# Seeding a PSUM bank with the first product, and a new order of the seven products, in a two-layer hybrid decoder

## The chip, the cores and the metric

One Trainium2 chip, all 8 cores. Each core runs the same program on one prompt sequence of 2048 tokens and 16 sample tokens (2064 columns); the cores share nothing but the memory. The metric is the device time of the slowest core in microseconds (us). Most executions agree within 0.3%. In some, one pair of cores or a whole die runs at a lower granted TensorE clock and the time is longer by some per cent or more; those runs are called slow and are not compared with anything here. A milder form, a pair of cores or a die at a clock of 0.97 to 0.98, still counts as fast in the ratios; it is named where it occurs, and there single stages are read from the undisturbed cores.

## The reference

Two layers of: half a SwiGLU feed-forward, a token mixer, half a second SwiGLU feed-forward. Only the feed-forwards are touched.

```python
D_MODEL, SEQ, BATCH, DEPTH, D_FF = 1024, 2048, 8, 2, 2816

def swiglu(x, w_gate, w_up, w_down):
    return (jax.nn.silu(x @ w_gate) * (x @ w_up)) @ w_down

def hybrid_layer(x, ...):
    h = x + 0.5 * swiglu(rms_norm(x, ffn1_norm), ffn1_w_gate, ffn1_w_up, ffn1_w_down)
    ...                                  # mixer: chunk MLP and short convolution, gated, h = h + m @ w_out
    h = h + 0.5 * swiglu(rms_norm(h, ffn2_norm), ffn2_w_gate, ffn2_w_up, ffn2_w_down)
    return h, new_buf, v
```

## The kernel before

The engines' names below: PE multiplies matrices, DVE and POOL work on vectors, ACT evaluates functions and copies. The token columns on a core make three pairs of blocks (344 + 344 columns). The 2816 hidden rows make 22 row blocks, in groups of 6, 8 and 8 ("groups 0, 1, 2").

**Gate and up.** For one row block and one pair of token blocks (a "unit"), gate and up for both token blocks form a 2 x 2 product of blocks. It is done as Strassen and Winograd do it, with seven products in place of eight. A product is four matmuls of 344 columns. Three PSUM banks y, z and w collect sums of products. A unit is spread over 17 slots; a new one begins every 7 slots, so at any time two to three are in flight and every slot has one product:

```python
t = 7 * u
put(t, begin)
put(t, lambda: (prod(1, "y", True), snap(ta, taR)))                     # ACT copies y to ta
put(t + 1, lambda: (prod(2, "z", True), add(ta, taR, "z"), free("z")))  # DVE: ta += z
put(t + 3, lambda: prod(7, "w", True))
put(t + 4, lambda: (prod(6, "y", False), snap(tb, tbR)))                # ACT copies y to tb
put(t + 9, lambda: (prod(5, "y", False), snap(tc, tcR)))                # ACT copies y to tc
put(t + 10, lambda: (add(tc, tcR, "w"), silu(ta, taR)))                 # DVE: tc += w; ACT: silu
put(t + 12, lambda: (prod(3, "y", False), out1(), free("y")))           # DVE: act = y * ta
put(t + 13, lambda: (prod(4, "w", False), end(), add(tb, tbR, "w"), free("w")))
put(t + 15, lambda: silu(tb, tbR))
put(t + 16, out2)                                                       # DVE: act = tc * tb
```

`end()` lets POOL make the weight differences (tiles T) of a later row block. Products 3, 5 and 6 use token differences (tiles S), products 4 to 6 weight differences (T). Product 7 uses one difference of each kind too, made in place: tokens in `nh` by DVE, weights in `ring` by POOL. In the rows of the profile, `pb` is a PSUM bank, `ring` the weights as loaded, `nh` the normed tokens and `D` the weight differences of the down-projection. `out2` has both inputs in SBUF; the other DVE operations of a unit have one in PSUM.

**Down.** The down-projections of groups 0 (three row pairs) and 1 (four row pairs) are also done with seven products, in three "thirds" (pairs of token blocks) of 14 steps (7 products, 2 halves of the output). DVE adds finished pairs of PSUM banks to h; four of the adds (three in the first third) go through an ACT copy and POOL instead. DVE also makes differences of activations (t3, t2 and two more) in every third. The down-projection of group 2 is plain.

```python
class Down:
    ORDER = ((1, "y", 0, 0), (2, "z", 0, 0), (7, "w", 4, 1), (6, "y", 4, 0), (4, "w", 4, 0), (5, "y", 4, 1), (3, "y", 0, 1))
    OTHER = ((2, 0), (7, 1), (4, 0), (3, 0))          # added by way of ACT and POOL
    ...
    def step(self, p, i, bank, blk, tok, dq, part=None):
        ...                                           # matmuls into the pair of banks
        add_half(tw[2], sz, hc, [tw[0][1], tw[1][1]] + hR, hR)   # DVE: h += half the pair
```

**Background work.** Norm work (squares on ACT, sums, normed tiles nh and token differences on DVE) is queued and let through at a fixed rate while the first units of a feed-forward run:

```python
if t % 7 in ((0, 3) if early and t < 84 else (2, 5)):
    bg.run(1)
```

Three stages, called "starts" here, have this load: group 0 of the second feed-forward of layer 0, of the first of layer 1, and of the second of layer 1 (start 1, 2, 3; at about 930, 1370 and 2270 us).

## Time and profile before

| | before |
|---|---|
| time, three runs beforehand | 2726.13 us (2725.81 to 2726.48) |
| PE busy | 97% of the span |
| DVE, ACT, POOL busy | 74%, 41%, 41% |
| PE time lost above the pace of its matmuls, in what the change touches | 69 us of 2722 |

A matmul of 344 columns starts 146 ns after the one before it when nothing holds PE up. So "stall" here always means: the distance between two starts in the trace, less that pace. From the same starts comes a ledger of stages, used throughout: a stage begins with its first matmul and ends where the next begins; the number is the median over the eight cores of one profiled execution. It is worked out from the trace, and is not a view of it. The ledger before, us:

```
beginning                                     116.2
start 1 / start 2 / start 3          78.4 / 81.5 / 78.8
gate/up of the other eight groups             806.3   ("regular")
very first down stage                          44.7
first thirds of the three later three-pair down stages   50.2
later thirds of the same                       85.8
four-pair down stages                         210.3
plain down, mixer, end                       1168.7
```

The rows of the profile that carry the reading are in the prediction below.

### The profile page before, as it was taken

To read this page: it belongs to the slowest core of one execution; us is meant where nothing else is said; L and a number is where in the kernel's file an instruction comes from. 1 tells how busy PE (TensorE), PEld (TensorE's weight loads), DVE (VectorE), ACT (ScalarE), POOL (GpSimd) and SP (SyncE) were. 2 spreads that over 40 slices of the span, in tenths; PEclk is the share of its full clock that TensorE was granted. 3 is DMA by queue.
4 is the path that set the end of the run, shared out by engine and by line. 5 is a ranking of instruction groups with operands and counts; after the bars stand their busy time and mean duration, and the time that the engine had idled before them with its cause. 6 is when DMAs were issued, how large, how long until landed. Compare 5 with 4: busy or idle time off the path is not lost.

```text
span 2722.9 us, 42526 instructions; the slowest of 8 cores (2718.5 to 2723.2 us)
## 1 busy us (share of the span) xinstructions
PE 2645.4 (97%) x16464; PEld 1592.5 (58%) x16464; DVE 2014.5 (74%) x3337; ACT 1113.3 (41%) x2188; POOL 1116.7 (41%) x1165
## 2 busy tenths in 40 slices
PE   8999999999999999999999999999999999999997
PEld 4466665566555565666555666646665555566664
DVE  5776667877787887676888676598768879866656
ACT  4244353523442443525353534453225224343356
POOL 1466536111221537563547646331112115575623
PEclk8999999999999999999999999999999999999999
DMA  7332323444364322222023313314444442232313
GB/s 173 47 47 34 49 36 65 70 71 70 57 101 75 60 41 45 40 47 43 13 32 47 62 25 60 69 32 78 71 70 76 82 74 37 47 55 32 55 32 125
DMA packets 87977, 159.66 MB, mean 59 GB/s; under 512 B 9376, under 2 KB 18464, under 8 KB 87488
## 3 DMA queue, kind: packets, MB, share of 16 engines
q0 software_dynamic: 74880, 136.35, 32.3%
q1 hardware_dynamic: 12464, 19.94, 2.3%
q8 instruction: 130, 2.13, 0.3%
q14 instruction: 71, 0.58, 0.1%
q10 hardware_dynamic: 432, 0.66, 0.1%
HBM read 284.49 MB, written 8.86 MB: 108 GB/s over the span
## 4 chain that ended last, share of the span: by engine, by line
PE 82%; DVE 13%; ACT 2%; issue 2%; POOL 1%; DMA 0%; SPq 0%; ACTq 0%; DVEq 0%; POOLq 0%
PE pb L288 45%; PE pb L284 37%; DVE h L266 3%; DVE nh L266 3%; DVE act L258 2%; DVE y L258 1%; ACT sq L246 1%; DVE acc L258 1%; DVE S L258 0%; DVE sq L258 0%; DMA h<-xT 0%; DVE tb L258 0%; DVE tc L258 0%; POOL sq L258 0%; DVE vb L258 0%
## 5 line engine op out<-in xcount | busy, mean ns | idle before, releaser
L272 POOL DMA_DIRECT2D ring<-wpk x456 | 247.5, 549 | 989.6 <-PE pb L284 529.6
L284 PE MATMUL pb<-nh,ring 128*128 128x384 f16 (+2 forms) x3360 | 607.8, 340 | 2.8 <-DVE nh L266 2.7
L288 PE MATMUL pb<-nh,ring 128*128 128x344 f16 x2952 | 510.4, 310 | 5.6 <-DVE nh L258 3.8
L284 PEld LDWEIGHTS pb<-nh,ring 128*128 128x128 f16 x3360 | 326.2, 98 | 258.1 <-issue 7.5
L266 DVE SCALAR_TENSOR_TENSOR h<-pb,h 128x688 f32<-128x688 f32 (+4 forms) x368 | 332.0, 911 | 136.4 <-PE pb L284 68.3
L288 PEld LDWEIGHTS pb<-nh,ring 128*128 128x128 f16 x2952 | 288.5, 98 | 150.1 <-DVE nh L258 4.8
L288 PE MATMUL pb<-S,T 128*128 128x344 f16 x1968 | 368.2, 310 | 3.8 <-POOL T L258 2.4
L288 PEld LDWEIGHTS pb<-S,T 128*128 128x128 f16 x1968 | 191.8, 98 | 100.8 <-POOL T L258 3.8
L246 ACT ACTIVATE ta<-pb 128x344 f32<-128x344 f32 x246 | 112.4, 457 | 321.2 <-PE pb L288 301.9
L258 DVE TENSOR_TENSOR ta<-pb,ta 128x344 f32<-128x344 f32 x246 | 126.8, 516 | 144.0 <-PE pb L288 142.1
L284 PE MATMUL pb<-act,ring 128*128 128x384 f16 (+3 forms) x1280 | 224.4, 336 | 3.0 <-DVE h L266 2.7
L288 PE MATMUL pb<-act,ring 128*128 128x344 f16 x1344 | 211.5, 310 | 12.2 <-DVE h L266 12.2
L258 DVE TENSOR_TENSOR act<-pb,ta 128x344 f16<-128x344 f32 x246 | 126.8, 515 | 127.0 <-PE pb L288 120.9
L258 POOL TENSOR_TENSOR T<-ring,T 128x512 f16<-128x512 f16 x164 | 212.7, 1297 | 12.9
L246 ACT ACTIVATE sq<-h 128x768 f32<-128x768 f32 (+3 forms) x140 | 121.7, 876 | 213.7 <-DVE h L266 193.8
L288 PE MATMUL pb<-nh,T 128*128 128x344 f16 x984 | 184.4, 310 | 11.5 <-DVE tc L258 7.1
L258 POOL TENSOR_TENSOR h<-h,cp 128x688 f32<-128x688 f32 x88 | 146.5, 1667 | 111.1 <-ACT cp L246 110.9
L266 DVE SCALAR_TENSOR_TENSOR nh<-h,cv,acc 128x384 f16<-128x384 f32 (+2 forms) x240 | 185.8, 816 | 7.1 <-ACT acc L246 3.6
L258 DVE TENSOR_TENSOR act<-tc,tb 128x344 f16<-128x344 f32 x246 | 181.0, 736 | 6.7 <-ACT tb L246 6.7
L288 PE MATMUL pb<-S,ring 128*128 128x344 f16 x984 | 184.4, 310 | 1.2 <-ACT tc L246 0.9
L284 PEld LDWEIGHTS pb<-act,ring 128*128 128x128 f16 x1280 | 123.5, 99 | 104.3 <-issue 9.6
L246 ACT ACTIVATE cp<-pb 128x688 f32<-128x688 f32 x88 | 65.4, 743 | 281.4 <-PE pb L288 281.4
(127 smaller groups left out, 3884.7 us busy)
## 6 DMA issues: line engine op xcount, KB each, us to landing
ring<-wpk POOLq DMA_DIRECT2D x456, 256.0 KB, 5.3
ext<-wpk POOLq DMA_DIRECT2D x64, 256.0 KB, 5.7
yT<-y SPq DMA_DIRECT2D x6, 768.0 KB, 3.6
h<-xT SPq DMA_DIRECT2D x4, 768.0 KB, 7.8
h<-xT SPq DMA_DIRECT2D x2, 1024.0 KB, 8.5
yT<-y SPq DMA_DIRECT2D x2, 1024.0 KB, 3.9
h<-xT SPq DMA_DIRECT2D x2, 800.0 KB, 8.1
h<-xT SPq DMA_DIRECT2D x4, 384.0 KB, 8.9
```

The lines of the kernel that those rows point to most:

```text
L246: return lambda e: e.activation(out=out, in_=in_, func=func, scale=scale)
L258: return lambda e: e.tensor_tensor(out=out, in0=in0, in1=in1, op=op)
L266: return lambda e: e.scalar_tensor_tensor(out=out, in0=in0, scalar=scalar, in1=in1, op0=op0, op1=op1)
L272: return lambda e: e.dma_start(out=out, in_=in_)
L284: return lambda e: e.matmul(out, lhsT=lhsT, rhs=rhs, start=start, stop=stop)
L288: return lambda e: e.matmul(out, lhsT=lhsT, rhs=rhs, start=start, stop=stop, skip_group_check=True)
```

## The change

Intent: take DVE work off. Product 1 is copied by ACT into bank z, before product 2 accumulates on it there, so the sum of products 1 and 2 arises in PSUM and DVE's add is gone. For this product 2 comes two slots later and product 7 takes its place. The third temporary tc is filled the other way round: bank w is copied soon after product 7, and y is added to it after product 5; product 4 comes before product 3. The down-projection gets the same seed and one read of h less. The silu now reads bank z early. Background work runs three times in seven slots, instead of twice, at the start of the first feed-forwards.

```diff
-                    put(t, lambda: (prod(1, "y", True), snap(ta, taR)))
-                    put(t + 1, lambda: (prod(2, "z", True), add(ta, taR, "z"), free("z")))
-                    put(t + 3, lambda: prod(7, "w", True))
-                    put(t + 4, lambda: (prod(6, "y", False), snap(tb, tbR)))
-                    put(t + 9, lambda: (prod(5, "y", False), snap(tc, tcR)))
-                    put(t + 10, lambda: (add(tc, tcR, "w"), silu(ta, taR)))
-                    put(t + 12, lambda: (prod(3, "y", False), out1(), free("y")))
-                    put(t + 13, lambda: (prod(4, "w", False), end(), add(tb, tbR, "w"), free("w")))
-                    put(t + 15, lambda: silu(tb, tbR))
+                    put(t, lambda: (prod(1, "y", True), seed()))
+                    put(t + 1, lambda: (prod(7, "w", True), snap(tc, tcR, "w")))
+                    put(t + 3, lambda: prod(2, "z", False))
+                    put(t + 4, lambda: (prod(6, "y", False), snap(tb, tbR, "y")))
+                    put(t + 5, lambda: (silu_z(), free("z")))
+                    put(t + 9, lambda: (prod(5, "y", False), add(tc, tcR, "y")))
+                    put(t + 12, lambda: (prod(4, "w", False), add(tb, tbR, "w"), free("w")))
+                    put(t + 13, lambda: (prod(3, "y", False), end(), out1(), free("y")))
+                    put(t + 14, lambda: silu(tb, tbR))
                     put(t + 16, out2)
...
+                    def seed():
+                        ...
+                        P.emit("act", i_act(z[:, 0:sz], bk[:, 0:sz], AF.Copy), reads=[bR], writes=[zR])
...
-                    if t % 7 in ((0, 3) if early and t < 84 else (2, 5)):
+                    if t % 7 in ((1, 3, 5) if early and t < 84 and pre == "ffn1" else (0, 3) if early and t < 84 else (2, 5)):
                         bg.run(1)
...
         class Down:
-            ORDER = ((1, "y", 0, 0), (2, "z", 0, 0), (7, "w", 4, 1), (6, "y", 4, 0), (4, "w", 4, 0), (5, "y", 4, 1), (3, "y", 0, 1))
-            OTHER = ((2, 0), (7, 1), (4, 0), (3, 0))
+            ORDER = ((1, 0), (1, 1), (2, 0), (7, 0), (6, 0), (2, 1), (6, 1), (7, 1), (4, 0), (4, 1), (5, 0), (5, 1), (3, 0), (3, 1))
+            OTHER = ((7, 1), (4, 0), (3, 0))
...
+                if i == 1:
+                    if dq == 0:
+                        self.seed(0)          # ACT: z = y, no add to h after product 1
...
+                elif (i, dq) == (7, 0):
+                    self.seed(1)
```

Cut: the helpers that prepare the differences t3 and t2 earlier, another order of POOL's differences for the down-projection, a DVE difference that moves from after product 7 to after product 2, the split step and the delayed add of the first third, which go, and renamings.

## The prediction

> **What bounds the kernel now.** I read the page first (busy shares, chain), then the groups by form, then the timeline around each idle piece of PE. Page, parts 1 and 4:
>
> ```profile
> PE 2645.4 (97%) x16464; PEld 1592.5 (58%) x16464; DVE 2014.5 (74%) x3337; ACT 1113.3 (41%) x2188; POOL 1116.7 (41%) x1165
> ...
> PE 82%; DVE 13%; ACT 2%; issue 2%; POOL 1%; DMA 0%; SPq 0%; ACTq 0%; DVEq 0%; POOLq 0%
> ```
>
> PE carries the span; DVE's 13% are the places where PE stood and waited. The groups by form show for whom, and what the disputed operations cost:
>
> ```profile
> L288 PE MATMUL pb<-act,ring 128*128 128x344 f16 x1344 | 211.0, 310 | 12.4 <-DVE h L266 12.2 <-DVE act L258 0.2
> L288 PE MATMUL pb<-nh,T 128*128 128x344 f16 x984 | 183.9, 309 | 11.4 <-DVE tc L258 6.8
> L288 PE MATMUL pb<-act,D 128*128 128x344 f16 x672 | 105.5, 310 | 10.9 <-DVE act L258 5.3 <-DVE h L266 4.5
> L258 DVE TENSOR_TENSOR ta<-pb,ta 128x344 f32<-128x344 f32 x246 | 126.8, 515 | 143.7 <-PE pb L288 141.7 <-ACT tb L246 1.0
> L266 DVE SCALAR_TENSOR_TENSOR h<-pb,h 128x688 f32<-128x688 f32 x248 | 214.0, 871 | 68.2 <-PE pb L288 66.1 <-POOL h L258 1.0
> L246 ACT ACTIVATE ta<-pb 128x344 f32<-128x344 f32 x246 | 112.4, 457 | 320.5 <-PE pb L288 303.7 <-DVE act L258 15.4
> L246 ACT ACTIVATE cp<-pb 128x688 f32<-128x688 f32 x88 | 65.4, 743 | 281.2 <-PE pb L288 281.2
> ```
>
> Modelled ends hide part of a stall, so I took starts from the timeline: the 9,240 matmuls of 344 columns start 146 ns apart (median). What lies above 146 ns is stall: 35 us in the two products up to the activation (gate/up, seven products for eight), 34 us in the down-projection done the same way. All other kinds of matmul, which the change does not touch, have some 36 us. So the change can win at most about 69 us (2.5%).
>
> The gate/up stall in its regular form, from the timeline:
>
> ```profile
> 1661.92 0.52 DVE L258 TENSOR_TENSOR ta<-pb,ta 128x344 f32<-128x344 f32 x1 [0.65 <-PE pb L288]
> ...
> 1662.35 1.40 DVE L258 TENSOR_TENSOR act<-tc,tb 128x344 f16<-128x344 f32 x1
> ...
> 1663.46 2.54 POOL L258 TENSOR_TENSOR T<-ring,T 128x512 f16<-128x512 f16 x2
> 1663.47 0.75 PE L288 MATMUL pb<-S,ring 128*128 128x344 f16 x4
> 1663.67 0.46 ACT L246 ACTIVATE tb<-pb 128x344 f32<-128x344 f32 x1 [0.33 <-PE pb L288]
> 1663.68 0.50 DVE L258 TENSOR_TENSOR tc<-pb,tc 128x344 f32<-128x344 f32 x1
> 1664.25 0.52 DVE L258 TENSOR_TENSOR act<-pb,ta 128x344 f16<-128x344 f32 x1
> 1664.33 0.74 PE L288 MATMUL pb<-nh,T 128*128 128x344 f16 x4
> ```
>
> The DVE product of two SBUF tiles takes 1.40 us beside POOL's weight differences; one unit later it takes 0.51. So the add that reads bank w (tc) ends late, and product 4, which accumulates into w, starts about 0.27 us late. This occurs once in three units, 41 times: 11.4 us. The down-projection, at a stage of three row pairs:
>
> ```profile
> 1015.88 0.87 DVE L266 SCALAR_TENSOR_TENSOR h<-pb,h 128x688 f32<-128x688 f32 x1
> 1016.67 0.69 DVE L258 TENSOR_TENSOR t<-act 128x1032 f16<-128x1032 f16 x1
> 1016.90 1.03 PE L288 MATMUL pb<-act,ring 128*128 128x344 f16 x6 [1.25 <-DVE h L266]
> ...
> 1034.79 1.31 DVE L258 TENSOR_TENSOR act<-act,t 128x1032 f16<-128x1032 f16 x1
> 1036.02 0.86 DVE L266 SCALAR_TENSOR_TENSOR h<-pb,h 128x688 f32<-128x688 f32 x1
> 1036.15 3.07 PE L288 MATMUL pb<-act,D 128*128 128x344 f16 x18 [0.62 <-DVE act L258]
> ```
>
> At the start all four PSUM pairs are held until DVE has added two of them to h; later DVE (ten adds of 0.87 and four differences of 0.69 to 1.4 us a third, against 14 steps x 6 x 146 ns = 12.3 us of PE) is itself about the limit. With four row pairs PE has 16.4 us a third, and only the start stalls.
>
> **What the Trainium skill says.** "SBUF — State Buffer", Who interferes with whom: a DVE instruction with two SBUF inputs contends with a GpSimd instruction that reads SBUF. The 0.51 against 1.40 us agrees. "TensorE: Matmul & The Clock Gate", Wait — 56ns, not 53.3ns?: warm matmuls follow at N / 2.4 GHz + 2.5 ns, so 145.8 ns for 344 columns; the trace has 146. "ScalarE: Activation LUTs", What ACT_TABLE_LOAD costs: 186 ns + 0.833 N without pointer operands, 473 ns for 344; the copies took 457. The same page says ACT to PSUM is faster than to SBUF, so a copy into PSUM should cost 0.46 us at most, and 0.74 us for 688.
>
> **The change part by part.** The matmuls stay: 16,396 in both built programs. Counted from the built programs:
> 1. Gate/up: the copy of product 1 goes into bank z instead of to SBUF, and product 2 accumulates on it. 246 DVE adds of 515 ns vanish: 126.8 us of DVE. ACT keeps its count (246 copies, and the silu now reads PSUM).
> 2. Down: the sum of products 1 and 2 is read once. DVE h adds 248 to 216: 32 x 0.871 = 28 us less. POOL adds 88 to 72, ACT copies 88 to 72, plus 48 seeds: ACT +32 x 0.74 = 24 us.
> 3. Product 7 comes right after product 1, product 2 two slots later; w is copied by ACT soon after product 7, and product 4 now meets it 11 slots later.
> 4. Four more table loads of 1.28 us each: a silu now comes before the norm roots at the start of the two second feed-forwards.
> 5. Background norm work three times in seven slots instead of two at the start of the first feed-forwards.
>
> DVE loses 155 of 2014 us, but DVE is not the sum that sets the end; only PE stalls count.
>
> Gate/up, regular units: p2 needs the seed. In time from the start of p1: p1 ends 0.58, ACT starts 0.2 after the last start slot (0.78), copies to 1.24; p2 comes at 3 x 0.584 = 1.75. No wait, with 0.44 us to spare. p4 no longer waits for tc; p3 needs the add on y, emitted three slots earlier: no wait. So the 41 x 0.275 = 11.4 us go.
>
> Gate/up at the starts (about 930, 1370 and 2270 us; together some 20 us): DVE is full there with norm work. Six or seven units before the deadline save 0.52 us each, 3 us a start, but p7 meets the deadline (difference of nh) two slots earlier (+1.2 us), and p2's seed queues behind the squares on ACT once: net 1.7 x 3 = 5 us. The late stalls after each start (p4 at 1000 to 1014 and alike) sum to 4 us and go with p4. The tc copy between p5 and p3 at the joints (3 x 0.275 + 4 x 0.13, and 1.06 at the last tail) wins 2.
>
> Down, by a hand schedule with the rows' durations and 0.2 us from a product's last slot to its reader. Four pairs (4 stages), now 1.1 + 0.56 + 0.13 = 1.8: product 7 takes the last unit's pair and waits for its output, about 1.0. Win 0.8 x 4 = 3. Three pairs (3 stages), first third now 2.4: about 1.0 + 0.3 + 0.13 + 0.25 = 1.7, win 0.7. The other thirds now 1.98 each: the new ones have seed 0.12, second seed 0.17 (it waits for DVE's read of z), w pair 0.26, copy 0.13, last y 0.25, together 0.94, plus about 0.5 from differences beside POOL: 1.45, win 0.5 each. Sum 1.7 x 3 = 5. The very first down stage, now 7.8: about 5.2, win 2.6. Together 11.
>
> Sum: 11.4 + 5 + 4 + 2 + 11 = 33 us, so 2726 - 33 = 2693 us.
>
> **The rivals.**
> (a) The seed becomes the wait. It lies on PE to ACT to PE, and ACT runs in order: the silu of tb stands before the seed and needs a DVE add. If DVE is late by over 0.5 us, PE stops at p2. In regular units DVE has over a microsecond free, which speaks against; at the starts it is full, which speaks for. All three starts and half of the down gain gone: -20 us only, 2706. If it hit every unit by 0.15 us (246 x 0.15 = 37), nothing would be left: 2726.
> (b) DVE was the true limit, and PE follows its 155 us. Then nearly all 69 us of stall go: 2660. Against it: most gate/up units show DVE idle 0.65 to 0.74 us before ta and before act.
> (c) In the down stage the second seed and the tighter difference before product 4 (two steps after product 2 instead of three) cost more than the saved add. Without POOL beside it my schedule gives 0.94 a third where now only 0.5 is lost. No gain there: 2704.
> (d) A PE pause of some microseconds halves the clock for a while: at 1401 us, after 1.96 and 2.10 us of stall, twelve matmuls came at 287 ns. Longer deadline stalls would add 1.5 us each, shorter ones remove them.
>
> **Range and chances.** Sure is only the p4 part with its late stalls, 15 us; everything together with the removal of the starts' stalls would be 46. So 2680 to 2707 should hold 8 times in 10. Faster by over 2% needs under 2672, more than 54 of the 69 us: 0.04. Slower by over 2% would take a stall in nearly every unit: 0.02. Within 2%: 0.94.
>
> **What would show it.** The row of 984 matmuls pb<-nh,T (product 4) should lose its DVE tc wait. The row of ACT pb<-pb 128x344 should have 246 at 0.46 us or less, and the product-2 group (pb<-nh,ring) should show almost no idle before it that ends with ACT; if it does, rival (a). DVE should fall to about 1860 us busy. In the down rows the waits for DVE h should fall from 17 to about 9 us, with new waits of 0.1 to 0.2 us that end with the seed on ACT. PE's stalls above 146 ns should fall from 69 to about 36 us. The prediction is wrong if that sum falls by under 20 or over 46 us, or if another engine ends the span.

## The result, and the profile after

| | before | after |
|---|---|---|
| fast runs, us | 2725.5 to 2728.5, and one of 2741.9 | 2709.3 to 2711.6 |
| median over all runs, slow ones included, us | 2741.91 (15 runs) | 2710.59 (12 runs) |
| ratio of fast runs, 95% interval | | 0.9934 (0.992 to 0.9948) |
| PE busy | 97% | 97% |
| DVE busy, us | 2014.5 | 1917.6 |
| ACT busy, us | 1113.3 | 1152.6 |

A ratio is the mean time of one kernel's fast runs over that of the other's from the same rounds, so not quite the ratio of the medians. The run of 2741.9 is among the fast ones in it; without that run the ratio of the means is 0.994. The change wins 0.6 to 0.7%, or 16 to 18 us of run time, and 15 us of span in the ledger. 33 us were predicted, and the measured 2710.59 us lies outside the range of 2680 to 2707.

The page of the kernel after, parts 1 and 4:

```profile
PE 2636.7 (97%) x16464; PEld 1595.1 (59%) x16464; DVE 1917.6 (71%) x3059; ACT 1152.6 (43%) x2224; POOL 1096.4 (40%) x1149
...
PE 83%; DVE 11%; POOL 2%; ACT 2%; issue 1%; DMA 1%; SPq 0%; POOLq 0%; ACTq 0%; DVEq 0%
```

DVE's part of the chain fell from 13 to 11%, but POOL gained 1%: waits changed hands. The groups by form, PE (after `|`: busy us and mean ns of one; then idle time of PE before them and what ended it):

```profile
L288 PE MATMUL pb<-nh,ring 128*128 128x344 f16 x2952 | 512.5, 309 | 14.5 <-ACT pb L246 7.2 <-DVE nh L258 4.6 <-POOL ring L258 2.6
...
L288 PE MATMUL pb<-act,ring 128*128 128x344 f16 x1344 | 213.2, 309 | 11.9 <-DVE act L258 5.5 <-DVE h L266 4.2 <-POOL ring L258 0.8
L288 PE MATMUL pb<-S,ring 128*128 128x344 f16 x984 | 183.8, 309 | 7.6 <-DVE tc L258 7.5
L288 PE MATMUL pb<-nh,T 128*128 128x344 f16 x984 | 183.6, 309 | 0.0
```

Product 4 (`nh,T`) lost all of its 11.4 us of waiting. But products 1, 2 and 7 (`nh,ring`) had 4.8 us before and now have 14.5, half of it ended by the seed (`ACT pb`); product 3 (`S,ring`) went from 1.2 to 7.6. In the down-projection the waits that end with DVE's adds to h fell from 16.7 us (12.2 + 4.5) to 6.0 (4.2, and 1.8 in the row `act,D`), further than the 9 that were announced. DVE and ACT, by form:

```profile
L258 DVE TENSOR_TENSOR act<-tc,tb 128x344 f16<-128x344 f32 x246 | 223.6, 909 | 3.1 <-ACT tb L246 2.7
L266 DVE SCALAR_TENSOR_TENSOR h<-pb,h 128x688 f32<-128x688 f32 x216 | 187.3, 872 | 83.4 <-PE pb L288 80.2 <-POOL h L258 3.1
```

```profile
L246 ACT ACTIVATE pb<-pb 128x344 f32<-128x344 f32 x246 | 108.9, 443 | 33.3 <-PE pb L288 6.9
...
L246 ACT ACTIVATE pb<-pb 128x688 f32<-128x688 f32 x48 | 34.9, 728 | 67.4 <-DVE h L266 48.9 <-PE pb L288 18.5
```

The 246 adds `ta<-pb,ta` are gone and the h adds are 216, as counted. The product of two SBUF tiles (`act<-tc,tb`) takes 909 ns in the mean, 736 before: 43 us of the 155 us saved on DVE were given back here. It runs beside POOL more often: on the two profiled cores 133 of the 246 overlap a POOL operation on tensors, 92 before, and the others take 0.51 to 0.52 us. That is most of why DVE fell to 1917.6 us and not to the announced 1860 or so; the rest was not traced. A seed takes 443 ns.

A regular unit after, in the timeline (start, duration, engine; the bracket is idle time before it and what ended it):

```profile
1655.15 1.87 DVE L258 TENSOR_TENSOR act<-tc,tb 128x344 f16<-128x344 f32 x1
...
1657.96 0.75 PE L288 MATMUL pb<-S,ring 128*128 128x344 f16 x4
...
1658.55 1.33 PE L288 MATMUL pb<-nh,ring 128*128 128x344 f16 x8
...
1659.33 0.44 ACT L246 ACTIVATE pb<-pb 128x344 f32<-128x344 f32 x1
...
1660.30 0.75 PE L288 MATMUL pb<-nh,ring 128*128 128x344 f16 x4
1660.50 0.52 DVE L258 TENSOR_TENSOR tc<-pb,tc 128x344 f32<-128x344 f32 x1 [0.74 <-PE pb L288]
```

Product 1 starts at 1658.55, the seed runs from 1659.33 to 1659.77, and product 2 starts at 1660.30: 0.78, 1.22 and 1.75 us after product 1, where 0.78, 1.24 and 1.75 were predicted. Even a DVE product of 1.87 us (1655.15) no longer holds up a matmul.

The ledger after, with the stall sums of the profiled cores:

```
                              before   after   differs  predicted    stall before -> after
starts 1, 2, 3 together        238.7   239.6     +0.9      -9          21.5 -> 27.7
regular gate/up                806.3   797.4     -8.9     -13.4        12.0 ->  0.6
very first down stage           44.7    44.3     -0.4      -2.6         7.9 ->  7.5
first thirds, three pairs       50.2    53.6     +3.4      -2.1         6.3 ->  9.2
later thirds, three pairs       85.8    79.5     -6.3      -3.0        12.2 ->  5.9
four-pair down stages          210.3   207.2     -3.1      -3.2         6.5 ->  4.0
plain down, mixer, end        1168.7  1168.7      0.0       0          (not touched)
```

"Predicted" takes the prediction's own terms: 11.4 + 2 for regular units and joints; 5 + 4 for the starts; 0.8 x 4, 0.7 x 3 and 0.5 x 6 for the down stages. The stall columns are of one core each (2 before, 7 after). Core 7 had the longest start 1 of all (82.1 us, where the median is 79.3); counted in the same way on all eight cores, the stall of the three starts has a median of about 21 us before and 22 after. The differences add up to -14.4, the predictions to -33.3. So the time that was missed lies in two places above all: the starts (9.9 us) and the first thirds (5.5 us).

### The profile page after: what moved, and what is told of

It is laid out like the page before. It is cut to its first block, busy times and chain, and to the rows that moved or that the text cites. A ratio compares the mean times of both kernels' runs of the same rounds, so it can differ in the third digit from the quotient of the medians.

```text
span 2710.2 us, 41818 instructions; the slowest of 8 cores (2705.0 to 2710.2 us)
## 1 busy us (share of the span) xinstructions
PE 2636.7 (97%) x16464; PEld 1595.1 (59%) x16464; DVE 1917.6 (71%) x3059; ACT 1152.6 (43%) x2224; POOL 1096.4 (40%) x1149
## 3 DMA queue, kind: packets, MB, share of 16 engines
q8 instruction: 130, 2.13, 0.3%
## 4 chain that ended last, share of the span: by engine, by line
PE 83%; DVE 11%; POOL 2%; ACT 2%; issue 1%; DMA 1%; SPq 0%; POOLq 0%; ACTq 0%; DVEq 0%
PE pb L288 45%; PE pb L284 38%; DVE h L266 3%; DVE nh L266 3%; DVE act L258 2%; DVE y L258 1%; ACT sq L246 1%; POOL T L258 1%; POOL sq L258 0%; POOL ring L258 0%; POOL acc L258 0%; DVE acc L258 0%; POOL D L258 0%; DMA h<-xT 0%; DVE vb L258 0%
## 5 line engine op out<-in xcount | busy, mean ns | idle before, releaser
L288 PE MATMUL pb<-nh,ring 128*128 128x344 f16 x2952 | 512.5, 309 | 14.5 <-ACT pb L246 7.2
L266 DVE SCALAR_TENSOR_TENSOR h<-pb,h 128x688 f32<-128x688 f32 (+3 forms) x336 | 305.2, 915 | 155.8 <-PE pb L288 80.2
L258 DVE TENSOR_TENSOR tb<-pb,tb 128x344 f32<-128x344 f32 x246 | 126.8, 515 | 244.2 <-PE pb L288 244.2
L246 ACT ACTIVATE tb<-pb 128x344 f32<-128x344 f32 x246 | 112.5, 457 | 308.0 <-PE pb L288 308.0
L258 DVE TENSOR_TENSOR act<-tc,tb 128x344 f16<-128x344 f32 x246 | 223.6, 909 | 3.1 <-ACT tb L246 2.7
L258 DVE TENSOR_TENSOR tc<-pb,tc 128x344 f32<-128x344 f32 x246 | 126.2, 513 | 134.1 <-PE pb L288 133.1
L246 ACT ACTIVATE pb<-pb 128x344 f32<-128x344 f32 (+1 forms) x294 | 143.9, 489 | 100.7 <-DVE h L266 48.9
L246 ACT ACTIVATE tb<-tb 128x344 f32<-128x344 f32 x246 | 120.6, 490 | 139.1 <-DVE tb L258 139.1
```

Of the source, the lines that this page charges most:

```text
L246: return lambda e: e.activation(out=out, in_=in_, func=func, scale=scale)
L258: return lambda e: e.tensor_tensor(out=out, in0=in0, in1=in1, op=op)
L266: return lambda e: e.scalar_tensor_tensor(out=out, in0=in0, scalar=scalar, in1=in1, op0=op0, op1=op1)
L288: return lambda e: e.matmul(out, lhsT=lhsT, rhs=rhs, start=start, stop=stop, skip_group_check=True)
```

## The experiments

First the parts, then the two places. Each kernel was correct, in every run.

### 1 and 2. Each half alone

`gate_only` has the new gate/up with the old down-projection, `down_only` the reverse.

```diff
gate_only, against the kernel after (and so on: all of class Down and its calls as before)
-            ORDER = ((1, 0), (1, 1), (2, 0), (7, 0), (6, 0), (2, 1), (6, 1), (7, 1), (4, 0), (4, 1), (5, 0), (5, 1), (3, 0), (3, 1))
+            ORDER = ((1, "y", 0, 0), (2, "z", 0, 0), (7, "w", 4, 1), (6, "y", 4, 0), (4, "w", 4, 0), (5, "y", 4, 1), (3, "y", 0, 1))
down_only: the same exchange the other way round, against the kernel before
```

> The gate/up part of the change alone (seeded bank z, product 7 early, new roles of w and y, background rate), with the down-projection of before. My theory after the result: the 41 regular stalls at product 4 (11 us) go, but the starts of the three late feed-forward blocks win nothing (stall 24.6 us before, 25.4 after), because the seed on ACT and the early product 7 bring new waits: 9 to 11 us faster than before. Rival, the prediction's sum: 20 us faster (11.4 + 5 + 4). Rival, the gain is all in the down-projection: within 3 us of before.

> The down-projection part alone (seed, order, t2 early), with the gate/up of before. Theory: later thirds with three row pairs win 1 us each (2.0 to 0.95 in the trace), the first thirds lose 1 us (DVE reads of h queue behind a DVE product[...]), four row pairs win 0.8: about 5 to 7 us faster. Rival (c) of the prediction: the second seed costs what the saved add wins, 0 to 2 us. Rival, the prediction's term: 11 us. If the parts are independent, gate_only plus down_only give the whole change's 15 to 16 us.

Measured in five rounds: `gate_only` 0.9966 (0.9953 to 0.998), fast runs 2715.4 to 2719.1 us (two slow); `down_only` 0.9977 (0.9965 to 0.999), 2719.1 to 2721.9 us. In the same rounds the kernel before took 2724.9 to 2728.1. So -9 and -6 us, together the -15 of the whole: the halves add, and neither takes from the other. The ledger says the same of the stages: regular 797.4 with `gate_only` and 805.9 with `down_only`; first thirds 49.7 and 53.2; later thirds 85.7 and 79.5.

### 3. The change of roles without the seed

What of the gate/up gain is the seed? `roles_only` is the kernel before with tc filled the other way and product 4 ahead of product 3. DVE keeps its 246 adds.

```diff
-                    put(t + 3, lambda: prod(7, "w", True))
+                    put(t + 3, lambda: (prod(7, "w", True), snap(tc, tcR, "w")))
-                    put(t + 9, lambda: (prod(5, "y", False), snap(tc, tcR)))
-                    put(t + 10, lambda: (add(tc, tcR, "w"), silu(ta, taR)))
-                    put(t + 12, lambda: (prod(3, "y", False), out1(), free("y")))
-                    put(t + 13, lambda: (prod(4, "w", False), end(), add(tb, tbR, "w"), free("w")))
+                    put(t + 9, lambda: (prod(5, "y", False), add(tc, tcR, "y")))
+                    put(t + 10, lambda: silu(ta, taR))
+                    put(t + 12, lambda: (prod(4, "w", False), add(tb, tbR, "w"), free("w")))
+                    put(t + 13, lambda: (prod(3, "y", False), end(), out1(), free("y")))
```

> Kernel before with one thing of gate/up: w is copied by ACT right after product 7 and the sum with y is added after product 5, and product 4 runs before product 3. No seed, the DVE add of product 2 stays, products 1, 2, 7 in the old places. Theory: the regular stall at product 4 goes without any seed, so it is as fast as gate_only or faster: 10 to 14 us faster than before. Rival: the gain needs the 127 us of DVE that the seed saves; then it is under half of gate_only's gain.

Measured: 0.9965 (0.9953 to 0.9978), 2715.6 to 2718.0 us. That is `gate_only`'s gain without the seed. Its ledger: regular 798.7 (797.4 with the seed), starts 78.3 / 82.0 / 77.8 (79.9 / 81.5 / 78.8). `gate_only` adds three things to it: the seed, the early product 7 and the background rate. Together they buy 1.3 us in all the regular units, and at the starts nothing that shows.

### 4 and 15. Giving the DVE time back

If DVE time is worth nothing in the regular units, 246 idle reads of the same size may be put in. `give_back` puts one after product 7, on bank w; `give_back2` puts it after out1, on bank y.

```diff
give_back
+                    def spend():
+                        bk, bR = st["w"]
+                        P.emit("dve", i_ts(tmp["d"][0][:, 0:sz], bk[:, 0:sz], 0.25, None, ALU.mult), reads=[bR], writes=[tmp["d"][1]])
-                    put(t + 1, lambda: (prod(7, "w", True), snap(tc, tcR, "w")))
+                    put(t + 1, lambda: (prod(7, "w", True), snap(tc, tcR, "w"), spend()))
give_back2: spend() on bank y instead
-                    put(t + 13, lambda: (prod(3, "y", False), end(), out1(), free("y")))
+                    put(t + 13, lambda: (prod(3, "y", False), end(), out1(), spend(), free("y")))
```

> The whole change, with one DVE instruction per unit added (246 reads of bank w of about 0.5 us into a tile that nobody reads), which gives back the 127 us that the seed takes off DVE. Theory: in the regular units DVE has the time free, and at the starts the wall is ACT's seed and POOL's weight differences, so at most 4 us slower than the change (about 2710 to 2714). Rival: DVE is the limit at the starts, then 3 times 7 units times 0.5 us or about 10 us slower (2720).

Measured: 1.0102 (1.0088 to 1.0116), 2753.3 to 2754.8 us (one slow), 44 us over the change, far outside what was expected. The timeline of `give_back` in a regular unit shows why (`td` is the added read):

```profile
1700.44 0.76 PE L288 MATMUL pb<-S,ring 128*128 128x344 f16 x4 [0.60 <-DVE tc L258]
...
1702.95 0.52 DVE L262 TENSOR_SCALAR td<-pb 128x344 f16<-128x344 f32 x1 [1.20 <-PE pb L288]
...
1703.39 0.51 DVE L258 TENSOR_TENSOR act<-tc,tb 128x344 f16<-128x344 f32 x1
1703.81 0.51 DVE L258 TENSOR_TENSOR tc<-pb,tc 128x344 f32<-128x344 f32 x1
```

The read stands in DVE's queue ahead of the product `act<-tc,tb`, which was ready much earlier, and makes it wait 1.20 us for product 7. Then the product and the add to tc are late, and product 3 stands. The groups of this run by form: product 3 waits 39 us in all.

```profile
L288 PE MATMUL pb<-S,ring 128*128 128x344 f16 x984 | 184.9, 310 | 39.3 <-DVE tc L258 39.0
```

So this run measured a place in the queue, not an amount of time, and says nothing of the theory. `give_back2` is meant to mend that. Its first run fell on a chip at low clock (below); this is the second one:

> give_back2 once more on a chip that is not slow throughout. Expected as there: the 246 DVE reads cost nothing in the regular units where DVE waits anyway (797 us stay) and 2 to 4 us at each start: 2714 to 2722. Rival, DVE time has no worth anywhere: within 2 us of the change (2710). Rival, it counts everywhere: 2730 or more.

Measured: fast runs 2726.8 to 2727.3 us (one slow), 16 us over the change (ratio to before 0.9969, interval 0.9872 to 1.0066, wide because a run of the kernel before took 2761.8). The ledger against the kernel after: regular +1.6; starts +3.2, +0.9, +3.2; first thirds +5.1; four pairs +1.5. DVE time is worth next to nothing in some 800 us of regular units, and counts at the starts: there the added waits end with DVE's add to tc (0.4 us before the read was added, 2.3 with it, median of the cores in start 1). The first thirds are another matter. Much of the wait there is for the added read itself, which also holds bank y for half a microsecond longer:

```profile
L288 PE MATMUL pb<-act,ring 128*128 128x344 f16 x1344 | 215.5, 311 | 12.0 <-DVE td L262 8.9 <-DVE h L266 0.9 <-POOL ring L258 0.8
```

So in the down stages this run, too, measures a place in part, and its 5.1 us are no price of DVE time.

### 5 to 7. The starts

Why did 9 us of expected gain not come? The waits of PE in start 1, timeline, before:

```profile
937.36 0.94 PE L284 MATMUL pb<-acc,onesm 128*128 128x400 f32 x2 [2.05 <-DVE acc L258]
...
945.18 0.74 PE L288 MATMUL pb<-nh,T 128*128 128x344 f16 x4 [0.98 <-DVE tc L258]
...
954.13 0.76 PE L288 MATMUL pb<-nh,T 128*128 128x344 f16 x4 [0.26 <-DVE tc L258]
...
961.37 0.76 PE L288 MATMUL pb<-nh,ring 128*128 128x344 f16 x4 [0.65 <-DVE nh L258]
```

After:

```profile
931.09 0.76 PE L288 MATMUL pb<-nh,ring 128*128 128x344 f16 x4 [1.17 <-ACT pb L246]
...
938.25 1.28 ACT L246 ACT_TABLE_LOAD   x1
...
940.79 0.76 PE L288 MATMUL pb<-nh,ring 128*128 128x344 f16 x4 [1.41 <-ACT pb L246]
...
953.07 1.66 POOL L258 TENSOR_TENSOR ring<-ring 128x512 f16<-128x512 f16 x1
...
954.78 1.17 PE L288 MATMUL pb<-nh,ring 128*128 128x344 f16 x4 [2.00 <-POOL ring L258]
...
962.31 0.76 PE L288 MATMUL pb<-nh,ring 128*128 128x344 f16 x4 [1.59 <-DVE nh L258]
```

On this core DVE's waits (acc, tc) are gone in start 1. In their place PE waits for the seed, which stands behind table loads and squares in ACT's queue (1.17 and 1.41 us); for a weight difference of POOL that product 7 now needs two slots sooner (2.00); and for the token difference nh at the deadline, also sooner (1.59 instead of 0.65). This is the slowest core, and not typical in all of it: read on all eight, the seed (1.4 to 2.9 us a start) and the deadline (1.6 to 2.0, before 0.4 to 0.9) are waited for in every pass of starts 1 and 3, POOL's difference in five of the sixteen (0.8 us, here 2.56 in two waits).

Start 2 is different. There the largest wait of the kernel after is still DVE's add to tc, now in front of product 3: 4.5 to 5.0 us on every core, before 0.5 to 2.7 in front of product 4. One of its four waits on the profiled core:

```profile
1384.83 0.76 PE L288 MATMUL pb<-S,ring 128*128 128x344 f16 x4 [1.72 <-DVE tc L258]
```

Three suspects, then: the four extra table loads, the early product 7, the seed.

`fewer_loads` moves the first unit's silu from t + 5 to t + 10 at starts 1 and 3, and so removes the four extra table loads (33 as before).

```diff
-                    put(t + 5, lambda: (silu_z(), free("z")))
+                    put(t + (10 if early and u == 0 and pre == "ffn2" else 5), lambda: (silu_z(), free("z")))
```

> The whole change, but at the start of the two second feed-forwards the first unit's silu comes after the norm roots, so ACT loads a table 33 times as before and not 37. Theory A: the four loads (1.28 us each) stand ahead of the seeds of the next units and make PE wait at product 2 (in the trace 1.57 us once at each of the two starts): 3 to 4 us faster than the change. Theory B: the loads lie in ACT's idle time and other waits take their place (POOL's weight differences and the difference of nh set the end of the start): within 1 us of the change.

Measured: 0.9938 (0.9922 to 0.9954), 2708.2 to 2711.9 us; starts 1 and 3 at 79.8 and 79.6, against 79.3 and 79.1 of the change. The table loads are not the cause. The waits for the seed did get shorter there (2.8 to 1.6 us in start 1, 2.5 to 1.5 in start 3, medians of the cores), and the starts did not: other waits took their place. So waits read from a trace do not add up to the time that their removal would win.

`early_p7` is `roles_only` with products 2 and 7 exchanged as in the change, but with no seed:

```diff
-                    put(t + 1, lambda: (prod(2, "z", True), add(ta, taR, "z"), free("z")))
-                    put(t + 3, lambda: (prod(7, "w", True), snap(tc, tcR, "w")))
+                    put(t + 3, lambda: (prod(2, "z", True), add(ta, taR, "z"), free("z")))
+                    put(t + 1, lambda: (prod(7, "w", True), snap(tc, tcR, "w")))
```

> roles_only with products 2 and 7 exchanged: product 7 two slots earlier as in the change, but no seed: bank z is started fresh and DVE adds it. The starts had 21.8 us of stall in roles_only and 27.1 in the change's gate/up. Theory A, the early product 7 meets POOL's weight differences and the difference of nh too soon: stall at the starts 25 to 28 us, 3 to 6 us slower than roles_only (2720 to 2723). Theory B, it is the seed and the ACT queue ahead of it: as roles_only, 22 us and 2717.

Measured: 2743.7, 2743.1, 2720.6 and 2740.2 us, ratio 1.0036 (0.9994 to 1.0078). The ratio is inconclusive: three of the four runs have a pair of cores at a clock of 0.98; in the profiled one that pair has spans of 2739 and 2742, the other six cores 2715 to 2721. The one undisturbed run, 2720.6, is 2.6 to 5.0 us above those of `roles_only`. On the six undisturbed cores of the profiled run the starts took 79.5 / 84.8 / 79.4, against 78.3 / 82.0 / 77.8 of `roles_only`. So the early product 7 costs about 1.2, 2.8 and 1.6 us. In start 2 the cores of the two runs do not overlap (84.2 to 86.8, 80.3 to 83.3); in the others they do, so there the size is less sure. Its timeline in start 1 has two waits of the change, for POOL's difference and for the deadline. It is of core 1, of the disturbed pair, but undisturbed core 5 has the same waits there; on the other five undisturbed cores POOL's wait is 0.8 us or absent and the deadline's 2.0 to 2.1:

```profile
948.44 0.76 PE L288 MATMUL pb<-nh,ring 128*128 128x344 f16 x4 [0.81 <-POOL ring L258]
...
954.69 0.76 PE L288 MATMUL pb<-nh,ring 128*128 128x344 f16 x4 [1.99 <-POOL ring L258]
...
960.54 0.76 PE L288 MATMUL pb<-nh,ring 128*128 128x344 f16 x4 [1.59 <-DVE nh L258]
```

`hybrid` is the change with the form of `roles_only` (late product 7, no seed) at all three starts, the new background rate kept.

> The change with the seed and the early product 7 only in the regular groups; the starts take the form of roles_only (fresh z, DVE add, product 7 in its old place). Theory: the starts go back from 27.7 to about 22 us of stall and nothing else moves: 2704 to 2706, 5 to 6 us faster than the change. Rival: the starts are set by DVE, then the 127/3 us of DVE work that come back there keep the time at 2710 or make it worse.

Measured: 0.9981 (0.9935 to 1.0027), three runs 2714.9 to 2716.1 us and one of 2735.9. Starts 1 and 3 fell to 78.0 and 77.9, start 2 rose to 89.6, so theory and rival were each right in one place. The timeline of `hybrid` in start 2:

```profile
1377.16 0.76 PE L288 MATMUL pb<-S,ring 128*128 128x344 f16 x4 [2.19 <-DVE tc L258]
...
1400.40 0.76 PE L288 MATMUL pb<-nh,ring 128*128 128x344 f16 x4 [2.88 <-ACT acc L247]
```

In time that is 5 us above the change (the run of 2735.9 has a pair of cores at 0.98). At starts 1 and 3 the old order without the seed is better by about 1 us. At start 2, with three pieces of background work in seven slots, DVE's adds are one thing too many.

### 16. The background rate

`old_rate` is the change with two pieces in seven slots, as before.

```diff
-                    if t % 7 in ((1, 3, 5) if early and t < 84 and pre == "ffn1" else (0, 3) if early and t < 84 else (2, 5)):
+                    if t % 7 in ((0, 3) if early and t < 84 else (2, 5)):
```

> old_rate once more. Theory A: background work twice instead of three times in seven slots meets the deadline of the start of the second layer's first feed-forward later: that start 84 to 87 us instead of 81.2, the rest as the change: 2713 to 2716. Rival: the rate only moves waits, the start stays within 1 us and the time at 2710.

Measured: two undisturbed runs of 2714.5 and 2713.8 us; two of 2736 (the profiled one with a whole die at 0.98, the other with a pair of cores), and two slow ones. Ratio 0.9949 (0.9836 to 1.0062). On the four undisturbed cores of the profiled run start 2 took 85.0 us (84.3 to 85.8) and the other stages were as in the change within 0.6 us: the new rate is worth 3 to 4 us, at start 2. The waits say the same: with the old rate PE waits 5.7 to 5.9 us there for nh at the deadline, with the new one 0.8 to 1.2.

Start 2 can now be told in steps: 82.0 in `roles_only`; +2.8 by the early product 7 (84.8); +0.2, which is nothing, by the seed (85.0); -3.8 by the rate (81.2, the change). Before it was 81.5. At starts 1 and 3 kernels with the changed form took 78.3 to 79.9 in different runs and those with the roles form 77.7 to 78.3, so steps of under 1 us are not told apart there.

### 8, 13 and 14. The first thirds

The first third of a three-pair down stage after, timeline:

```profile
1011.37 1.88 DVE L258 TENSOR_TENSOR act<-act 128x1032 f16<-128x1032 f16 x1
...
1013.18 1.46 DVE L258 TENSOR_TENSOR act<-tc,tb 128x344 f16<-128x344 f32 x1
...
1017.36 2.13 DVE L258 TENSOR_TENSOR act<-tc,tb 128x344 f16<-128x344 f32 x1
...
1017.94 1.17 POOL L258 TENSOR_TENSOR T<-ring 128x512 f16<-128x512 f16 x1
...
1019.42 2.42 DVE L266 SCALAR_TENSOR_TENSOR h<-pb,h 128x688 f32<-128x688 f32 x3
...
1020.59 2.87 POOL L258 TENSOR_TENSOR T<-ring,T 128x512 f16<-128x512 f16 x2
...
1021.90 2.94 PE L288 MATMUL pb<-act,ring 128*128 128x344 f16 x18 [1.40 <-DVE h L266]
```

The last gate/up units still end while the down stage begins. POOL makes weight differences of the next group (T) at that time, and the last product of two SBUF tiles takes 2.13 us where it takes 0.51 alone. The adds to h then come late, and the step that needs their bank waits 1.40 us. Two ways out were tried. `late_out2` moves that last product behind the seventh step of the down stage, where the copy tiles are now set up too (cut below), to see whether its place counts:

```diff
+                    if len(self.steps) == 35:
+                        if self.post:
+                            self.post.pop()()
...
-                    put(t + 16, out2)
+                    if fill and tmp["seven"] and u == many - 1:
+                        tmp["seven"].post.append(out2)
+                    else:
+                        put(t + 16, out2)
```

> The change, with the last unit's product of two SBUF tiles on DVE (2.1 us beside POOL at the start of the down stage) emitted after product 6 of the first third instead of before the reads of h. Theory: the 1.56 us wait at product 7's second half (DVE's reads queue behind it) goes at the three stages with three row pairs, stall of the first thirds from 9.2 to about 5 us: 3 to 5 us faster than the change. Rival: the queue is only moved, and the difference before product 5 waits instead: within 1.5 us.

Measured: fast runs 2711.6 and 2712.9 us (two slow), 0.9945 (0.9924 to 0.9967); first thirds 54.9. No gain. The wait at the step is gone and another stands in its place, which the move itself made: the ACT copy (`cp`), whose tile lies in the space of the unit's temporaries, now waits for the moved DVE product.

```profile
1021.64 1.38 ACT L246 ACTIVATE cp<-pb 128x688 f32<-128x688 f32 x2 [6.18 <-DVE act L258]
1022.44 1.05 PE L288 MATMUL pb<-act,ring 128*128 128x344 f16 x6 [1.16 <-ACT cp L246]
```

`no_T` leaves DVE as it is and takes POOL away: the last unit before a down stage does not start the differences T, which come a third later, as many in number.

```diff
                     def end():
-                        wx.ahead()
+                        if not (fill and tmp["seven"] and u == many - 1):
+                            wx.ahead()
                         down_sums()
```

> no_T once more, since all cores of its chip ran at a clock of 0.94 in that call. Expected, as there: POOL's weight differences start in the second third of the down stage instead of ahead of it, DVE's product of two SBUF tiles takes 0.5 to 0.7 us there instead of 2.1; the three first thirds with three row pairs go from 53.6 us (the change) to 49 to 51, the later thirds stay at 79.5: 2706 to 2708. Rival: DVE's queue is long without POOL: 53 us and 2710.

Measured: fast runs 2705.4 and 2704.8 us (two slow, so no interval), before 2725.3 to 2729.0 in the same rounds. First thirds 53.6 to 49.2, later thirds 79.5 as before: 5 us less than the change. The same place in its timeline:

```profile
1015.29 0.51 DVE L258 TENSOR_TENSOR act<-tc,tb 128x344 f16<-128x344 f32 x1
...
1015.84 2.62 DVE L266 SCALAR_TENSOR_TENSOR h<-pb,h 128x688 f32<-128x688 f32 x3
...
1018.53 2.93 PE L288 MATMUL pb<-act,ring 128*128 128x344 f16 x18
```

The product takes 0.51 us again, and the step has no wait of note before it. This settles the first thirds: what was lost there is DVE beside POOL, at one moment.

`best` joins the two findings: `no_T`, and the form of `roles_only` at starts 1 and 3 alone.

> no_T together with the starts of the second feed-forwards in the form of roles_only (fresh bank z, DVE add, product 7 in its old place, 33 table loads); the start of the first feed-forward keeps the seed and the faster rate. Theory: these two starts go from 79.3 and 79.1 us (the change) to about 78, the rest as no_T: 2 to 3 us faster than no_T_again, 2703 to 2706, the fastest of all. Rival: the starts are set by POOL's weight differences and the norm work whatever the form: as no_T_again within 1 us.

Measured: 0.9912 (0.9896 to 0.9929), 2702.9 to 2703.5 us (one slow), the fastest of all: 24 us below the kernel before and 7 below the change. Starts 77.7 / 81.4 / 77.9, first thirds 49.0.

### 9 to 12. Four runs on a chip at low clock

The first runs of `old_rate`, `give_back2`, `no_T`, and a `late_out2b` (which also orders the two copy tiles the other way) came to a chip where both dies had a granted clock of about 0.94 and the kernel before itself took 2860.6 to 2873.8 us.

```diff
late_out2b, against late_out2
+                self.copy.reverse()
```

> The whole change, with the background norm work at the start of the second layer's first feed-forward again twice in seven slots. The start takes 81.2 us in the change and 81.5 in before. Theory A: the faster rate does the work that the deadline (difference of nh) waits for earlier, so the start becomes 2 to 4 us longer here. Theory B: the rate fills DVE so that its adds come late (1.3 to 1.9 us waits for tc); the start becomes 1 to 3 us shorter here. Nothing else moves.

> The whole change plus one 0.5 us DVE read of PSUM per unit, as give_back, but placed after the output product on bank y, where DVE waits for nothing new. give_back was 44 us slower than the change because its read stood in DVE's queue before the product of two SBUF tiles and made it wait for product 7. Theory: DVE's time has no worth in the regular units (0 there), and up to 3 us at each start: 2 to 9 us slower than the change (2712 to 2719). Rival, DVE time counts everywhere: 20 us or more.

> The change, but POOL does not start the next group's weight differences in the last unit ahead of the down stages; they come inside the second third, as in before. Theory: [...]DVE's last product of two SBUF tiles takes 0.5 to 0.7 us instead of 2.1 and the differences 0.7, so the 1.56 us wait of the first thirds with three row pairs shrinks by 1 us or more each; the later thirds get it back in part (before lost 1.5 us there by the same collision, the new order has more room): 2 to 4 us faster in the first thirds, 0 to 2 us slower in the later ones. Rival: the queue of DVE is long by its own count of instructions and POOL matters little: within 0.5 us per third.

> late_out2 removed the 1.56 us wait but made the copy after product 7 wait for the moved DVE instruction (1.16 us), since that copy's buffer lies on its inputs; here the copy takes the other buffer first. Theory: that wait goes, and a late difference before product 4 beside POOL's weight differences (0.55) stays: first thirds 52 to 53 us for three instead of 53.6, 1 to 2 us faster than the change. Rival: another wait takes its place, no change.

Measured, runs not marked slow: `old_rate` 2860.5 to 2878.3, `give_back2` 2873.7 to 2880.8 (ratio 1.0025), `no_T` 2841.6 and 2856.3, `late_out2b` 2868.7 to 2879.7 (ratio 1.0016). The spread within one kernel there is as large as what was asked, so nothing is concluded from them. Three were run again (above). `late_out2b` was not, and is open; `no_T` made it needless.

## Why the prediction was right or wrong

**Right: the bound and the regular units.** The 41 waits of product 4 were the stall of the regular units: 12.0 us became 0.6. (The 11.4 us of idle time in product 4's row are not the same 11.4: over 6 of them lie at the starts, and the row hides part of the regular stall, which only the starts of matmuls show.) The stage won 8.9 us, not the 13.4 with joints. At the joints, where 2 us were to be won, time was lost: the role change makes the plain down-projection wait for the last activation. The row of its matmuls, before and then after:

```profile
L284 PE MATMUL pb<-act,ring 128*128 128x384 f16 x768 | 128.8, 328 | 0.4
```

```profile
L284 PE MATMUL pb<-act,ring 128*128 128x384 f16 x768 | 129.6, 329 | 2.1 <-DVE act L258 2.1
```

That is 1.7 us (`roles_only` has the same 2.1). Of the 4.5 us that are missing, 2.0 not won and 1.7 lost are at joints, and 0.8 is not accounted for.

**Wrong: the starts, 9.9 of the 18.9 us missed.** The step that failed is "net 1.7 x 3 = 5 us", together with the late stalls that "sum to 4 us and go with p4". Of the 3 us that DVE saves a start, it took off 1.2 for product 7, which leaves 0.1 for the seed's queueing on ACT. The kernels between give the sum of the three starts step by step (medians of the undisturbed cores of one profiled run each, so steps of under 1 us are within the spread):

| step | predicted | measured |
|---|---|---|
| change of roles, late stalls (`roles_only`) | -4 | -0.6 (238.7 to 238.1) |
| early product 7 (`early_p7`) | +3.6 | +5.6 (243.7) |
| seed, with the DVE time that it saves, and the rest of the change but the rate (`old_rate_again`) | -8.7 | -1.3 (242.4) |
| background rate (the change) | not priced | -2.8 (239.6) |

So the largest miss is the seed. DVE's saved time is real (`give_back2` puts 7.3 us on it at the three starts) and was paid away at the same starts: on the profiled core the seed stands behind ACT's other work three times in start 1 (1.17, 0.25 and 1.41 us), twice in start 2 (0.49 and 0.92) and three times in start 3 (1.28, 0.25 and 1.41), rather than once; these eight waits are the whole 7.2 us of the row. The early product 7 costs more than was priced, above all at start 2, where it meets the deadline of nh: 5.7 to 6.3 us of waiting, 0.6 to 1.8 in `roles_only`; on some cores it waits for POOL's differences too, which the prediction had not looked at. And when the late stalls went, other waits took most of their place: in `roles_only` the waits for tc at the starts fell from 6.5 to 3.9 us (medians), the starts by 0.6.

**Wrong: the first thirds, 5.5 us.** The step "about 1.0 + 0.3 + 0.13 + 0.25 = 1.7, win 0.7" had no allowance for DVE beside POOL; the prediction made one for the other thirds only. Measured, the stalls went up from 6.3 to 9.2 us over the three stages; without POOL's T differences at that moment the first thirds take 49.2 us, 1.0 less than before.

**Wrong in size: the very first down stage.** 2.6 us were expected and 0.4 came. PE waits there 0.94 us for a weight difference of POOL, 1.70 for t2 and 1.96 for an add to h. No experiment was made on it.

**Better than predicted: the later thirds.** 6.3 us against 3.0. The hand schedule's sum without POOL, 0.94 us a third, was measured as 0.11 + 0.20 + 0.26 + 0.12 + 0.26 = 0.95; the 0.5 us added on top of it for POOL was under 0.1. The allowance for POOL was in the wrong third.

**Right: the four-pair stages**, 3.1 against 3.2 us.

**The rivals.** (a), the seed as the wait, was right at the starts in that the seed ate the DVE gain there, and wrong in the regular units, where the margin was as worked out. (b), DVE as the true limit everywhere, is refuted by `roles_only`, which has the gain without the saving; in start 2 of the kernel after, DVE's add to tc does end the largest wait. (c), no gain in the down stage, was wrong in the later thirds. (d), the halved clock after a pause, was seen again: after the 2.00 us wait at 954.78 four matmuls took 1.17 us instead of 0.76, and the starts of eleven came 286 to 287 ns apart. The announced sign, stall falling from 69 to 36 us, came out as 66.4 to 54.9 in the stages of the ledger above, a fall of 12 us; the prediction had named a fall of under 20 as its refutation. Its count of 16,396 matmuls is not that of the traces, which have 16,464 before and after, so that the number did stay the same.

## What to carry to other kernels

Taking work off an engine pays only at the places where that engine ends the wait; read those places one by one, and for each ask which other engine's deadline the new order brings nearer. An order that is right for the steady state can be wrong for the starts and joints, and it costs little to give those their own order: here 2 us at two starts. Another 5 us came from moving POOL's work away from a moment at which DVE needs two SBUF tiles. When an operation is put in to measure what time is worth, it must stand in the queue where its inputs are already there and hold nothing that others wait for, or it measures its place.

## What the Trainium skill lacked or had wrong

- "PSUM — Partial Sum Buffer", the summary table's row on seeded accumulation, says that the seed must be 0. Its own section The four PSUM rules is more exact: a matmul that does not clear adds onto engine-written data where an earlier matmul has written the element. Here each core seeded a bank 246 times and a pair of banks 48 times with a nonzero product (443 and 728 ns each) and every run was correct; matmuls had written the banks before. The row is stricter than the section. The section's warning stands untested, that where a bit was left clear a seed is overwritten and only 0 is safe either way.
- "SBUF — State Buffer", Who interferes with whom, says that a DVE instruction with two SBUF inputs contends with GpSimd's reads. It gives no durations for it. Here the 344-column f32 product took 0.51 us alone and, in the lines shown, 1.40 to 2.13 us beside POOL's differences (1.12 and 1.24 us in the mean of all that overlap POOL, before and after), the 1032-column f16 difference 0.69 and 1.88 us; DVE operations with one input in PSUM stayed at 0.50 to 0.52.
- "TensorE: Matmul & The Clock Gate", What's actually happening, puts the return to the slow clock after an idle window of about 3.4 us. Here shorter pauses were enough at times: on the eight cores of the profiled run after, 344-column matmuls came 286 to 287 ns apart after 4 of the 52 pauses of 1.84 to 2.34 us between two starts, and not after the other 48. When a pause is enough was not worked out.
- No page works out what this prediction got wrong most: when work moves from one in-order engine to another, its wait is set by what stands ahead of it in the new queue. Here the seed, 0.44 us long, was waited for 7.2 us in sum on the profiled core, in eight waits, all at the starts.
